# One-column steps, low parts on GpSimd and the order of work at the ends of sub-layers, in a two-layer fp32 trunk on one core

## The chip, the core and the metric

The kernel runs on one core of a Trainium2 chip. A core has TensorE (matrix products; the profile lists its weight loads apart, as PEld), VectorE (DVE), ScalarE (ACT), GpSimd (POOL) and SyncE (SP), which issues DMAs. SBUF is the memory of 128 partitions that the engines work in; PSUM is the one that TensorE accumulates in. The metric is the device time of one execution in microseconds. A VectorE operation that takes a tensor and, for each partition, one number from a column of SBUF is called a tensor-scalar step here; `scalar_tensor_tensor` takes two tensors and such a scalar.

## The reference

The input is 256 frames of 2048 numbers, all fp32. Four sub-layers follow each other, each of the form x <- x + RMSNorm_post(f(RMSNorm_pre(x))):

```python
for layer in range(DEPTH):                       # DEPTH = 2
    h = rms_norm(x, mix_pre_g[layer])
    m = pool_conformer_mixer(...) if layer % 2 == 0 else short_conv_mixer(...)
    x = x + rms_norm(m, mix_post_g[layer])
    h = rms_norm(x, ffn_pre_g[layer])
    x = x + rms_norm(sq_relu_mlp(h, ffn_w1[layer], ffn_w2[layer]), ffn_post_g[layer])
```

rms_norm is y = x * rsqrt(mean(x*x) + 1e-6) * g. The first mixer projects to 3072 columns, pools and convolves over time and projects back with `ab_w_out`; the second projects to 6144 columns, convolves over three frames between two gates and projects back with `sc_w_out`. The MLP is (relu(h W1))^2 W2 with 8192 hidden columns. Most of the work is these products with fp32 weights, which are read from HBM once.

## The kernel before

**Tiling.** The 256 frames are two row blocks, t = 0 and 1, of 128 rows on the partitions. A product works on an output block of 512 columns: one PSUM bank `pg`, into which TensorE sums over the 128-row slices k of the contraction. The left operand of a matmul is a slice of the transposed input, the right one 512 columns of a weight.

**Split products.** Weights and inputs are split into a high part of fewer bits and the rest. For each k three matmuls are issued: high weight by high input (line 216), low weight by high input (217), high weight by low input (218). Such a loop over the 16 slices of a segment (one weight block of 2048 x 512, eight loads) is 48 matmuls for each row block.

**Weight stream.** `prep_to` (lines 166 to 176) brings the weights in, two slices k at a time: a DMA on SyncE into `raw` (four buffers), a cast on ScalarE into `whi`, and the subtraction raw - whi (line 174) into `wlo`, nine buffers each. The subtraction runs on VectorE; for the first nine loads of the three segments that open MLP 0, mixer 1 and MLP 1 (`f1_0_0_0`, `sC0`, `f1_1_0_0`), which `pool_lo` holds, on GpSimd. A load waits until the low part that read its buffer four loads earlier is done.

**End of a sub-layer.** The output blocks of a row block are evacuated from PSUM one by one. In the mixers `mix_evac` sums the squares on ScalarE (line 555) and multiplies by the gain of the post-norm (`gp`, an own DMA) on VectorE (line 556); in the first mixer two blocks are added from halves first (line 611). In the MLP the eight groups of hidden columns are added up in SBUF (line 664), and the last addition is followed by the squares and the product with the gain (lines 669, 671). Then `mix_close` and `rsqrt` make the scale of the row on [128, 1] columns: a reduction and a step (269, 561), `scalar_tensor_tensor` of the last square sum with the others (564), a root on ScalarE and a reciprocal (289), and one Newton step for it (291, 292, 293). `close_row` adds scale times block to the residual x in four pieces (line 319) and queues, behind some more slices of matrix products (`later`), `norm_chunk` for each of the four pieces: four transposes on TensorE (line 245), the high part `xh` on ScalarE (231), the low part `xl` on VectorE (234). These eight-slice buffers `xh`, `xl` are the left operands of the next sub-layer's first segment, which row block 0 enters as soon as row block 1's last block is done. A "chunk" below is one of these four pieces, k = 0 to 3, 4 to 7, 8 to 11, 12 to 15. Each row's pre-norm scale `rr` is worked out later (`row_scale`) and applied when the products leave PSUM.

**Order of the work.** The kernel is written for one stream of instructions on each engine, each in order; the framework's scheduler simulates a timeline of the program as it is built and sets the order in which the instructions of an engine stand from the order of the code, their priority and the simulated times. An engine waits at the head of its queue until the inputs are there; SyncE's DMAs are in such a queue too.

## Time and profile before

| | before |
|---|---|
| median of 3 runs | 2096.06 us (2094.62 to 2098.18) |
| span of the profiled execution | 2096.0 us |
| TensorE (PE) busy | 2048.8 us, 98%, 9253 instructions |
| VectorE (DVE) busy | 1187.4 us, 57% |
| ScalarE (ACT) busy | 1007.8 us, 48% |
| GpSimd (POOL) busy | 221.5 us, 11% |
| bytes moved by DMA | 390.31 MB, mean 186 GB/s |
| TensorE's mean granted clock | 0.992 |

The profile is that of one execution, whose own time is its span; times in it count from its first instruction. A row says on which engine and line of the kernel something ran and on which tiles (the numbers behind their names are left out). Where an engine stood idle, the row behind names what ended the wait, as far as the semaphores show it. A matmul of 512 columns is shown with a length of 0.39 us while the next one starts before it has ended, so a busy share of TensorE near 100% says that it hardly waits. The granted clock is that share of full speed at which TensorE was allowed to run.

### The profile page before, as it was taken

The numbers are of one execution on the slowest core, as the hardware profiler recorded it, in microseconds if no ns is written. First come the engines' busy times: TensorE is split into PE (matmuls) and PEld (weight loads), VectorE is DVE, ScalarE is ACT, GpSimd is POOL, SyncE is SP. The second block draws the span as 40 slices with busy tenths as digits, with TensorE's granted clock in tenths as the row PEclk, the third lists the DMA queues.
The fourth block names the chain that finished last, engine by engine and source line by source line (L and its number), as shares of the span: only waits on it lengthen the run. The fifth ranks groups of instructions, "written<-read, shape, count | busy, mean of one in ns | idle before, by whom it ended". The sixth has DMA issues, their size and how long they took to land.

```text
span 2096.0 us, 24559 instructions
## 1 busy us (share of the span) xinstructions
PE 2048.8 (98%) x9253; PEld 1693.0 (81%) x9253; DVE 1187.4 (57%) x1494; ACT 1007.8 (48%) x1296; POOL 221.5 (11%) x111
## 2 busy tenths in 40 slices
PE   8999889999999999999999999989999999999998
PEld 7888778888888888887788888878888888888886
DVE  4787765445454555546655655565455454454545
ACT  7454565445344354444643444465444444354443
POOL 5886210000000000002100000220000000000000
PEclk9999999999999999999999999999999999999999
DMA  7665445556565555555555565546556565565553
GB/s 259 197 208 174 151 161 191 190 171 206 196 196 171 196 186 196 189 173 170 174 199 180 182 204 181 191 156 212 180 178 211 174 201 186 175 202 199 192 170 120
DMA packets 203079, 390.31 MB, mean 186 GB/s; under 512 B 12368, under 2 KB 14512, under 8 KB 202960
## 3 DMA queue, kind: packets, MB, share of 16 engines
q1 hardware_dynamic: 202656, 388.55, 56.3%
q8 instruction: 72, 1.18, 0.2%
q14 instruction: 47, 0.39, 0.1%
q0 software_dynamic: 256, 0.18, 0.0%
q10 hardware_dynamic: 48, 0.02, 0.0%
HBM read 386.60 MB, written 2.10 MB: 185 GB/s over the span
## 4 chain that ended last, share of the span: by engine, by line
PE 84%; DVE 3%; DMA 1%; ACT 0%; issue 0%; DVEq 0%; SPq 0%; ACTq 0%
PE pg L218 27%; PE pg L216 27%; PE pg L217 27%; PE pt L245 2%; DVE x L319 1%; DVE sm L291 0%; DVE sm L293 0%; DMA gp<-in_mix_post_g_dram 0%; DMA raw<-in_ab_w_out_dram 0%; DVE sm L564 0%; DMA raw<-in_ffn_w_dram 0%; DMA raw<-in_sc_w_in_dram 0%; DVE m L556 0%; ACT whi L173 0%; DVE m L671 0%
## 5 line engine op out<-in xcount | busy, mean ns | idle before, releaser
L174 DVE TENSOR_TENSOR wlo<-raw,whi 128x1024 fp32r<-128x1024 f32 x633 | 775.4, 1227 | 583.9 <-ACT whi L173 550.3
L173 ACT CAST whi<-raw 128x1024 fp32r<-128x1024 f32 x722 | 760.1, 1054 | 581.8 <-PE pg L218 381.8
L218 PE MATMUL pg<-whi,xl 128*128 128x512 f32 x1568 | 618.5, 395 | 17.9 <-DVE xl L234 17.9
L216 PE MATMUL pg<-whi,xh 128*128 128x512 f32 x1568 | 612.6, 392 | 1.3 <-ACT xh L231 0.7
L217 PE MATMUL pg<-wlo,xh 128*128 128x512 f32 x1568 | 612.2, 391 | 0.0
L217 PE MATMUL pg<-wlo,ah 128*128 128x512 f32 x1024 | 399.2, 390 | 0.0
L216 PE MATMUL pg<-whi,ah 128*128 128x512 f32 x1024 | 398.7, 389 | 0.0
L218 PE MATMUL pg<-whi,al 128*128 128x512 f32 x1024 | 398.2, 391 | 0.0
L218 PEld LDWEIGHTS pg<-whi,xl 128*128 128x128 f32 x1568 | 295.8, 189 | 79.0 <-DVE xl L234 20.1
L217 PEld LDWEIGHTS pg<-wlo,xh 128*128 128x128 f32 x1568 | 295.8, 189 | 61.7
L216 PEld LDWEIGHTS pg<-whi,xh 128*128 128x128 f32 x1568 | 295.9, 189 | 61.1 <-ACT xh L231 1.7
L174 POOL TENSOR_TENSOR wlo<-raw,whi 128x1024 fp32r<-128x1024 f32 x89 | 214.3, 2435 | 1012.4 <-DVE wlo L174 693.8
L217 PEld LDWEIGHTS pg<-wlo,ah 128*128 128x128 f32 x1024 | 192.6, 188 | 40.2
L216 PEld LDWEIGHTS pg<-whi,ah 128*128 128x128 f32 x1024 | 192.6, 188 | 39.5
L218 PEld LDWEIGHTS pg<-whi,al 128*128 128x128 f32 x1024 | 192.5, 188 | 39.3
L634 ACT ACTIVATE t<-pg,rr 128x512 f32<-128x512 f32 x64 | 43.8, 685 | 190.6 <-PE pg L218 190.6
L664 DVE TENSOR_TENSOR m<-pg,m 128x512 f32<-128x512 f32 x112 | 76.9, 686 | 89.4 <-PE pg L218 89.4
L216 PE MATMUL pg<-whi,yh 128*128 128x512 f32 x256 | 101.2, 396 | 1.6 <-ACT yh L240 1.5
L217 PE MATMUL pg<-wlo,yh 128*128 128x512 f32 x256 | 100.9, 394 | 0.0
L218 PE MATMUL pg<-whi,yl 128*128 128x512 f32 x256 | 98.8, 391 | 0.2 <-DVE yl L241 0.2
L385 DVE SCALAR_TENSOR_TENSOR acc<-pp,par,acc 128x256 f32<-128x256 f32 x240 | 96.3, 479 | 0.1
L241 DVE TENSOR_TENSOR al<-pt,ah 128x512 fp32r<-128x512 f32 x64 | 44.0, 687 | 71.8 <-ACT ah L240 71.7
(124 smaller groups left out, 858.8 us busy)
## 6 DMA issues: line engine op xcount, KB each, us to landing
raw<-in_ffn_w_dram SPq DMA_DIRECT2D x512, 512.0 KB, 4.7
raw<-in_sc_w_in_dram SPq DMA_DIRECT2D x96, 512.0 KB, 4.8
raw<-in_ab_w_in_dram SPq DMA_DIRECT2D x48, 512.0 KB, 4.4
raw<-in_ab_w_out_dram SPq DMA_DIRECT2D x32, 512.0 KB, 3.9
raw<-in_sc_w_out_dram SPq DMA_DIRECT2D x32, 512.0 KB, 5.4
x<-in_x_dram SPq DMA_DIRECT2D x8, 256.0 KB, 7.7
gp<-in_mix_post_g_dram SPq DMA_DIRECT2D x8, 256.0 KB, 6.2
gp<-in_ffn_post_g_dram SPq DMA_DIRECT2D x8, 256.0 KB, 4.3
```

What stands on the lines that cost most here:

```text
L173: act.copy(hi, raw)
L174: (pool if nxt[0] in pool_lo else lo_eng[0](nxt[0])).tensor_tensor(lo, raw, hi.bitcast(F32), ALU.subtract)
L216: pe.matmul(ps, lh, wh, start=start and k == 0, stop=False)
L217: pe.matmul(ps, lh, wl, start=False, stop=False)
L218: pe.matmul(ps, ll, wh, start=False, stop=stop and k == n - 1)
L241: dve.tensor_tensor(lo, src, hi.bitcast(F32), ALU.subtract)
L245: pe.transpose(p[:, j * P : (j + 1) * P], src[:, j * P : (j + 1) * P], ident)
L319: dve.scalar_tensor_tensor(xs[t][:, cs], ms[t][:, cs], s, xs[t][:, cs], ALU.mult, ALU.add)
L385: dve.scalar_tensor_tensor(a, src, wcol, a, ALU.mult, ALU.add)
L634: act.activation(rl, ps, AF.Relu, scale=rr[t])
L664: dve.tensor_tensor(dst, ps, dst, ALU.add)
```

## The change

Five things are changed; the computation is the same.

- Lines 564, 291 and 293, one-column steps of two SBUF tensors, become tensor-scalar steps whose other operand is a scalar column (600, 322, 324 in the new numbering).
- `pool_lo` holds every second load of the three opening segments (four of the first eight or nine), and such a low part is worked out in two instructions of 512 columns; the other loads' low parts run on VectorE.
- The last group of an MLP block is added up in PSUM, squared from PSUM and multiplied from PSUM into SBUF (`last_evac`). The program's very last product, which was on GpSimd, is on VectorE too.
- `urgent` gives the instructions of the evacuation, of `mix_close` with the residual sums, and of `norm_chunk` a priority of 150 over the others, which the scheduler heeds.
- In the first segment behind each of the three ends, row block 0 runs through `mms_wide`: high by high and high by low for all k first (lines 240, 241), then low by high for all k (248).

```diff
     for key in ("f1_0_0_0", "sC0", "f1_1_0_0"):
-        pool_lo |= set(range(seg[key][0], seg[key][0] + 9))
+        pool_lo |= set(seg[key][1::2])
     wt = {}
...
             act.copy(hi, raw)
-            (pool if nxt[0] in pool_lo else lo_eng[0](nxt[0])).tensor_tensor(lo, raw, hi.bitcast(F32), ALU.subtract)
-            wt[nxt[0]] = (hi, lo)
+            i_, on_pool = nxt[0], nxt[0] in pool_lo
+            def low(raw=raw, hi=hi, lo=lo, on_pool=on_pool, eng=lo_eng[0](i_)):
+                for s in ((slice(0, CB), slice(CB, 2 * CB)) if on_pool else (slice(None),)):
+                    (pool if on_pool else eng).tensor_tensor(
+                        lo[:, s], raw[:, s], hi.bitcast(F32)[:, s], ALU.subtract)
+            low()
+            wt[i_] = (hi, lo)
             nxt[0] += 1
...
     AHEAD = 8
+    URGENT = 150
...
+    def mms_wide(ps, lhs, ids):
+        n = 2 * len(ids)
+        prep_to(ids[-1])
+        for i, c in enumerate(ids):
+            if i == n // 4:
+                tick()
+            for j in range(2):
+                k = 2 * i + j
+                wh = wt[c][0][:, j * CB : (j + 1) * CB]
+                lh, ll = lhs(k)
+                pe.matmul(ps, lh, wh, start=k == 0, stop=False)
+                pe.matmul(ps, ll, wh, start=False, stop=False)
+        tick()
+        for i, c in enumerate(ids):
+            if i == n // 4:
+                tick()
+            for j in range(2):
+                k = 2 * i + j
+                pe.matmul(ps, lhs(k)[0], wt[c][1][:, j * CB : (j + 1) * CB],
+                          start=False, stop=k == n - 1)
+        tick()
     def ahead(ids, t):
...
         h = small()
-        dve.scalar_tensor_tensor(h, y, v, y, ALU.mult, ALU.mult)
+        dve.tensor_scalar(h, y, v, y, ALU.mult, ALU.mult)
         dve.tensor_scalar(h, h, -0.5, 1.5, ALU.mult, ALU.add)
-        dve.tensor_tensor(y, y, h, ALU.mult)
+        dve.tensor_scalar(y, y, h, None, ALU.mult)
         return y
...
     ms, rr, nparts = {}, {}, {}
+    def urgent(fn, *args):
+        with tc.high_priority(URGENT):
+            fn(*args)
...
             else:
-                later(2 + (c + 1) // 2, lambda c=c: norm_chunk(t, c, *nxt_gain))
-
+                later(2 + (c + 1) // 2, lambda c=c: urgent(norm_chunk, t, c, *nxt_gain))
     for t in range(NT):
...
         v = small()
-        dve.scalar_tensor_tensor(v, last, 1.0 / D, base, ALU.mult, ALU.add)
+        dve.tensor_scalar(v, last, 1.0 / D, base, ALU.mult, ALU.add)
         r = rsqrt(v, root=lambda s: act.activation(s, last, AF.Sqrt, bias=base, scale=1.0 / D))
...
             ps = o
-        mix_evac(t, cb, ps, gps[cb], parts)
+        urgent(mix_evac, t, cb, ps, gps[cb], parts)
         if cb == 1:
-            mix_close(t, parts, ("ffn_pre", 0))
-
+            urgent(mix_close, t, parts, ("ffn_pre", 0))
+    def last_evac(t, cb, ps, gp, parts):
+        dst = ms[t][:, cb * CB : (cb + 1) * CB]
+        dve.tensor_tensor(ps, ps, dst, ALU.add)
+        junk = tp.tile([P, CB], BF16, tag="junk", name=nm("junk"), bufs=2)
+        act.activation(junk, ps, AF.Square, accum_out=parts[t][:, cb : cb + 1])
+        dve.tensor_tensor(dst, ps, gp, ALU.mult)
     def ffn(l, nxt_gain, final=False):
...
                     ps = psg()
-                    mms(ps, lhs_x(t), ids, 0, True, True)
+                    if (e, c, t) == (0, 0, 0):
+                        mms_wide(ps, lhs_x(t), ids)
+                    else:
+                        mms(ps, lhs_x(t), ids, 0, True, True)
                     rl = t512()
...
                     continue
-                dve.tensor_tensor(dst, ps, dst, ALU.add)
-                if last:
-                    if cb not in gps:
-                        gps[cb] = post_gain(ffn_post_g, l, cb)
-                    junk = tp.tile([P, CB], BF16, tag="junk", name=nm("junk"), bufs=2)
-                    act.activation(junk, dst, AF.Square, accum_out=parts[t][:, cb : cb + 1])
-                    eng = pool if final and (cb, t) == (NCB - 1, NT - 1) else dve
-                    eng.tensor_tensor(dst, dst, gps[cb], ALU.mult)
-                    if cb == NCB - 1:
-                        mix_close(t, parts, nxt_gain, final)
+                if not last:
+                    dve.tensor_tensor(dst, ps, dst, ALU.add)
+                    continue
+                if cb not in gps:
+                    gps[cb] = post_gain(ffn_post_g, l, cb)
+                urgent(last_evac, t, cb, ps, gps[cb], parts)
+                if cb == NCB - 1:
+                    urgent(mix_close, t, parts, nxt_gain, final)
...
                 ps = psg()
-                mms(ps, lhs_x(t), ids, 0, True, True)
+                if (j, key, t) == (0, "C", 0):
+                    mms_wide(ps, lhs_x(t), ids)
+                else:
+                    mms(ps, lhs_x(t), ids, 0, True, True)
                 if key == "C":
...
             mms(ps, lhs_y(t), ids, 0, True, True)
-            mix_evac(t, cb, ps, gp, parts)
+            urgent(mix_evac, t, cb, ps, gp, parts)
             if cb == NCB - 1:
-                mix_close(t, parts, ("ffn_pre", KT))
+                urgent(mix_close, t, parts, ("ffn_pre", KT))
```

The names in the order below are tiles with their numbers. VectorE at the end of the first mixer, before: the last product of row block 0 (`m_2077`), its root's steps, the four residual sums (`x_85`), then row block 1 (`m_2078`) and the first `xl` of MLP 0.

```order
L556 TENSOR_TENSOR m_2077<-opart_1807,gp_2294 128x512
L564 SCALAR_TENSOR_TENSOR sm_2353<-parts_2075,sm_2349 128x1
L289 RECIPROCAL sm_2357<-sm_2355 128x1
L291 SCALAR_TENSOR_TENSOR sm_2359<-sm_2357,sm_2353 128x1
L292 TENSOR_SCALAR sm_2359<-sm_2359 128x1
L293 TENSOR_TENSOR sm_2357<-sm_2357,sm_2359 128x1
L319 SCALAR_TENSOR_TENSOR x_85<-m_2077,sm_2357,x_85 128x512 x4
L611 TENSOR_TENSOR opart_1810<-pg_2371,opart_1810 128x512
L556 TENSOR_TENSOR m_2078<-opart_1810,gp_2263 128x512
L269 TENSOR_REDUCE sm_2506<-parts_2076 128x1
L561 TENSOR_SCALAR sm_2505<-sm_2506 128x1
L234 SCALAR_TENSOR_TENSOR xl_2364<-pt_2396,par,xh_2363 128x128 x4
```

The same place after, in two pieces that follow each other:

```order
L600 TENSOR_SCALAR sm_2355<-parts_2075,sm_2351 128x1
L320 RECIPROCAL sm_2359<-sm_2357 128x1
L322 TENSOR_SCALAR sm_2361<-sm_2359,sm_2355 128x1
L323 TENSOR_SCALAR sm_2361<-sm_2361 128x1
L324 TENSOR_SCALAR sm_2359<-sm_2359,sm_2361 128x1
L178 TENSOR_TENSOR wlo_2312<-raw_2309,whi_2311 128x1024
L355 SCALAR_TENSOR_TENSOR x_85<-m_2077,sm_2359,x_85 128x512 x4
L647 TENSOR_TENSOR opart_1810<-pg_2373,opart_1810 128x512
L178 TENSOR_TENSOR wlo_2418<-raw_2415,whi_2417 128x1024
```

```order
L592 TENSOR_TENSOR m_2078<-opart_1810,gp_2263 128x512
L300 TENSOR_REDUCE sm_2510<-parts_2076 128x1
L597 TENSOR_SCALAR sm_2509<-sm_2510 128x1
L178 TENSOR_TENSOR wlo_2431<-raw_2428,whi_2430 128x1024
L647 TENSOR_TENSOR opart_1810<-pg_2441,opart_1810 128x512
L265 SCALAR_TENSOR_TENSOR xl_2366<-pt_2398,par,xh_2365 128x128 x4
L592 TENSOR_TENSOR m_2078<-opart_1810,gp_2294 128x512
L265 SCALAR_TENSOR_TENSOR xl_2366<-pt_2454,par,xh_2365 128x128 x4
L178 TENSOR_TENSOR wlo_2542<-raw_2539,whi_2541 128x1024
L600 TENSOR_SCALAR sm_2513<-parts_2076,sm_2509 128x1
L265 SCALAR_TENSOR_TENSOR xl_2368<-pt_2467,par,xh_2367 128x128 x4
```

Between the root's steps and the low parts of chunk 0 (`xl_2366` from `pt_2398`), of chunk 1 (from `pt_2454`) and of chunk 2 (`xl_2368`) there are now four low parts of weights (`wlo_...`), and the three one-column steps carry the new operation.

TensorE where MLP 0's first segment begins, before: three matmuls for each slice k.

```order
L216 MATMUL pg_2559<-whi_2298,xh_2363 128x512
L217 MATMUL pg_2559<-wlo_2299,xh_2363 128x512
L218 MATMUL pg_2559<-whi_2298,xl_2364 128x512
L216 MATMUL pg_2559<-whi_2304,xh_2363 128x512
L217 MATMUL pg_2559<-wlo_2305,xh_2363 128x512
L218 MATMUL pg_2559<-whi_2304,xl_2364 128x512
L216 MATMUL pg_2559<-whi_2304,xh_2363 128x512
L217 MATMUL pg_2559<-wlo_2305,xh_2363 128x512
L245 MATMUL pt_2463<-ident,x_85 128x128 x4
L218 MATMUL pg_2559<-whi_2304,xl_2364 128x512
```

The same after: two for each slice, the low parts of the weights not yet among them.

```order
L240 MATMUL pg_2563<-whi_2298,xh_2365 128x512
L241 MATMUL pg_2563<-whi_2298,xl_2366 128x512
L240 MATMUL pg_2563<-whi_2298,xh_2365 128x512
L241 MATMUL pg_2563<-whi_2298,xl_2366 128x512
L240 MATMUL pg_2563<-whi_2304,xh_2365 128x512
L241 MATMUL pg_2563<-whi_2304,xl_2366 128x512
L240 MATMUL pg_2563<-whi_2304,xh_2365 128x512
L276 MATMUL pt_2467<-ident,x_85 128x128 x4
L241 MATMUL pg_2563<-whi_2304,xl_2366 128x512
L240 MATMUL pg_2563<-whi_2311,xh_2365 128x512
```

The transposes of chunk 2 (`pt_2463`, `pt_2467`) stand behind eight matmuls before and behind seven after; by then the matmuls have come to the third slice k in one case and to the fourth in the other.

SyncE behind the first end, before: weight loads (`raw_...`) and the loads of the next post-norm gain (`gp_...`).

```order
L170 DMA raw_2425<-in_ffn_w_dram 128x2x512
L304 DMA gp_7499<-in_ffn_post_g_dram 128x512
L170 DMA raw_2431<-in_ffn_w_dram 128x2x512
L170 DMA raw_2535<-in_ffn_w_dram 128x2x512
L304 DMA gp_7554<-in_ffn_post_g_dram 128x512
```

After:

```order
L170 DMA raw_2428<-in_ffn_w_dram 128x2x512
L170 DMA raw_2434<-in_ffn_w_dram 128x2x512
L170 DMA raw_2539<-in_ffn_w_dram 128x2x512
L340 DMA gp_7502<-in_ffn_post_g_dram 128x512
L170 DMA raw_2545<-in_ffn_w_dram 128x2x512
```

The first gain load stands behind two weight loads more than before.

## Rows read from the trace of the kernel before

**Rows 1.** The list of waits of TensorE over the whole span: engine and line that waited <- what it waited for: us in total, times, longest.

```profile
PE pg L218 <- DVE xl L234: 17.9, 5, 7.3
PE pt L245 <- DVE x L319: 7.7, 3, 4.2
```

**Rows 2.** Busy time of the engines in three windows (us from the span's start), at the ends of the first three sub-layers. Columns: window, its length, then busy us and instructions of PE, PEld, DVE, ACT and POOL, the granted TensorE clock as a share of full speed, the DMA engines' share, GB/s.

```profile
256.00:310.00 54.00, 43.57 (x188) 34.81 (x187) 40.21 (x77) 30.87 (x73) 14.29 (x6) 0.91 0.47 152
970.00:1035.00 65.00, 56.39 (x246) 45.12 (x245) 47.89 (x87) 37.11 (x83) 21.92 (x11) 0.95 0.52 163
1340.00:1410.00 70.00, 62.72 (x288) 51.47 (x287) 47.59 (x80) 39.98 (x84) 22.94 (x9) 0.95 0.55 174
```

**Rows 3.** The same three windows, the transposes of line 245 alone (PE and PEld busy us and instructions, clock, DMA share, GB/s).

```profile
256.00:310.00 54.00, 6.62 (x36) 5.44 (x36) 0.91 0.47 152
970.00:1035.00 65.00, 5.31 (x32) 4.13 (x32) 0.95 0.52 163
1340.00:1410.00 70.00, 5.99 (x40) 5.05 (x40) 0.95 0.55 174
```

**Rows 4.** The timeline of TensorE around the first end and, for the transposes, around the third. Columns: start us, us, engine, line, operation, out<-in, count [idle time before it <- what ended it]; "x4" is four instructions shown as one row, from the start of the first to the end of the last. Matmuls are pipelined, so the distance from start to start, not the length, is what one takes.

```profile
236.66 0.39 PE L217 MATMUL pg<-wlo,yh 128*128 128x512 f32 x1
...
246.86 0.39 PE L217 MATMUL pg<-wlo,yh 128*128 128x512 f32 x1
...
279.54 0.80 PE L218 MATMUL pg<-whi,xl 128*128 128x512 f32 x1 [5.71 <-DVE xl L234]
280.13 0.63 PE L216 MATMUL pg<-whi,xh 128*128 128x512 f32 x1
280.56 0.63 PE L217 MATMUL pg<-wlo,xh 128*128 128x512 f32 x1
...
1358.58 0.60 PE L245 MATMUL pt<-ident,x 128*128 128x128 f32 x4
...
1359.24 0.39 PE L218 MATMUL pg<-whi,yl 128*128 128x512 f32 x1
```

**Rows 5.** The timeline of VectorE at the first end, same columns.

```profile
248.19 0.69 DVE L611 TENSOR_TENSOR opart<-pg,opart 128x512 f32<-128x512 f32 x1 [1.02 <-PE pg L218]
251.06 2.60 DVE L556 TENSOR_TENSOR m<-opart,gp 128x512 f32<-128x512 f32 x1 [2.18 <-DMA gp<-in_mix_post_g_dram]
253.59 2.35 DVE L564 SCALAR_TENSOR_TENSOR sm<-parts,sm 128x1 f32<-128x1 f32 x1
...
256.05 2.22 DVE L291 SCALAR_TENSOR_TENSOR sm<-sm,sm 128x1 f32<-128x1 f32 x1
258.30 0.15 DVE L292 TENSOR_SCALAR sm<-sm 128x1 f32<-128x1 f32 x1
258.49 2.08 DVE L293 TENSOR_TENSOR sm<-sm,sm 128x1 f32<-128x1 f32 x1
260.60 2.74 DVE L319 SCALAR_TENSOR_TENSOR x<-m,sm,x 128x512 f32<-128x512 f32 x4
```

**Rows 6.** The timeline of GpSimd at the first end, same columns.

```profile
250.72 9.84 POOL L174 TENSOR_TENSOR wlo<-raw,whi 128x1024 fp32r<-128x1024 f32 x4 [4.34 <-ACT whi L173]
```

**Rows 7.** The timeline of VectorE at the second end, same columns.

```profile
978.68 0.69 DVE L664 TENSOR_TENSOR m<-pg,m 128x512 f32<-128x512 f32 x1 [1.53 <-PE pg L218]
...
981.56 2.12 DVE L291 SCALAR_TENSOR_TENSOR sm<-sm,sm 128x1 f32<-128x1 f32 x1
...
986.08 6.91 DVE L319 SCALAR_TENSOR_TENSOR x<-m,sm,x 128x512 f32<-128x512 f32 x4
```

**Rows 8.** The timeline of VectorE at the third end, same columns.

```profile
1353.34 9.16 DVE L319 SCALAR_TENSOR_TENSOR x<-m,sm,x 128x512 f32<-128x512 f32 x4
```

**Rows 9.** All instructions of line 383, grouped: duration in ns as minimum/median/maximum, first and last start, form.

```profile
L383 DVE TENSOR_SCALAR acc<-pp,par x8: 537/544/547, 65.8 to 124.3; 128x256 f32<-128x256 f32 x8
```

**Rows 10.** The page: line 174 on VectorE and on GpSimd among the costliest groups (count | busy us, mean ns of one | idle before, releaser), and the loads of the MLP weights among the DMA issues (count, KB each, median us from issue to landing).

```profile
L174 DVE TENSOR_TENSOR wlo<-raw,whi 128x1024 fp32r<-128x1024 f32 x633 | 775.4, 1227 | 583.9 <-ACT whi L173 550.3
...
L174 POOL TENSOR_TENSOR wlo<-raw,whi 128x1024 fp32r<-128x1024 f32 x89 | 214.3, 2435 | 1012.4 <-DVE wlo L174 693.8
...
raw<-in_ffn_w_dram SPq DMA_DIRECT2D x512, 512.0 KB, 4.7
```

**Rows 11.** The timeline of ScalarE at the first end, columns as in rows 4.

```profile
270.79 1.05 ACT L173 CAST whi<-raw 128x1024 fp32r<-128x1024 f32 x1 [2.14 <-DMA raw<-in_ffn_w_dram]
271.74 0.62 ACT L555 ACTIVATE junk<-opart 128x512 bf16<-128x512 f32 x1
```

**Rows 12.** The timeline of SyncE's DMA issues at the first end (a row lasts from the first issue to the last).

```profile
264.69 0.34 SPq L304 DMA_DIRECT2D gp<-in_ffn_post_g_dram  x1
265.13 0.90 SPq L170 DMA_DIRECT2D raw<-in_ffn_w_dram  x2
```

**Rows 13.** The timeline of TensorE at the second end, columns as in rows 4.

```profile
996.75 0.50 PE L218 MATMUL pg<-whi,xl 128*128 128x512 f32 x1 [0.43 <-DVE xl L234]
...
1008.44 0.59 PE L218 MATMUL pg<-whi,xl 128*128 128x512 f32 x1 [4.06 <-DVE xl L234]
```

**Rows 14.** The timeline of TensorE at the third end.

```profile
1362.65 0.39 PE L216 MATMUL pg<-whi,xh 128*128 128x512 f32 x1
...
1376.95 0.79 PE L218 MATMUL pg<-whi,xl 128*128 128x512 f32 x1 [7.28 <-DVE xl L234]
```

**Rows 15.** The timeline of VectorE at the program's end.

```profile
2088.13 0.85 DVE L291 SCALAR_TENSOR_TENSOR sm<-sm,sm 128x1 f32<-128x1 f32 x1
```

## The prediction

> **What bounds the kernel now.** I read first the page's busy shares, then who waits for whom on TensorE, then the three stretches in which it waits, and last what VectorE does there. TensorE is busy 98% of the span and its chain is nearly the whole program, so only its idle and slow time can be won. The list of its waits shows two large groups [rows 1]: 17.9 us for `xl` of VectorE line 234 (the low part of the next sub-layer's input) and 7.7 us for `x` of line 319 (the residual sum). All of it lies where one sub-layer closes and the next begins: mixer 0 to MLP 0 (first end, near 255 us), MLP 0 to mixer 1 (second, near 985), mixer 1 to MLP 1 (third, near 1360).
>
> What these ends lose in all is the length of their stretches less the matmuls at full speed. A 512-column matmul takes 0.227 us from start to start (45 from 236.66 to 246.86), and four transposes add 0.44 (0.66 from the four to the second matmul behind them, less 0.227) [rows 4]. With the counts of [rows 2, 3]: 54.0 - 152 x 0.227 - 9 x 0.44 = 15.5; 65.0 - 214 x 0.227 - 8 x 0.44 = 12.9; 70.0 - 248 x 0.227 - 10 x 0.44 = 9.3. Sum 37.7 us: the 25.6 of waits, and the rest the clock. Behind the wait that ends at 279.54 the matmuls start 0.43 apart, the lower of the two clock levels [rows 4].
>
> Why VectorE is late: at the first end a one-column step with two SBUF tensors takes 2.35, 2.22 and 2.08 us, while the one-input step between them takes 0.15 [rows 5]. GpSimd runs four low parts of 2.4 us back to back at that time [rows 6], and each slow step ends where one of these ends. So a VectorE instruction with two SBUF inputs waits out the GpSimd instruction that is running. The same shows in the residual sums: four take 2.74 without GpSimd [rows 5], 6.91 and 9.16 with it [rows 7, 8].
>
> **The change, part by part.** *One-column steps.* Lines 564, 291, 293 become one-input steps with the other columns as scalars. Line 383 has that form (one SBUF tensor, two column scalars) and all eight ran in 0.54 us for 256 columns, spread from 65.8 to 124.3 us [rows 9]; 0.15 is the row for a column. I take 0.15 to 0.22. Bounds: 0.15 and the 2.35 of today. At the first end that takes 6.1 us out of row block 0's chain (2.35 + 2.22 + 2.08 - 0.52), at the second about 3.9 (two steps like the 2.12 at 981.56 [rows 7]).
>
> *Four low parts on GpSimd, each in halves.* GpSimd's 2.44 us [rows 10] becomes two instructions; by their size, 1.2 each is my estimate. What a residual sum still waits is thus at most 1.2, not 2.4. But five of nine low parts go to VectorE at 1.23 each [rows 10], and the order shows four of them between the root and the `xl` of chunks 0 to 2, on the very engine that TensorE waits for.
>
> *MLP blocks summed in PSUM.* Line 671 read two SBUF tensors; the new product reads PSUM and one SBUF tensor, a form of 0.69 (line 611 in [rows 5], 664 in [rows 7]). The sum is of the same form as before. Cover: nothing waits for the product but the residual sum; it costs nothing more than now.
>
> *Chain first.* The transposes of row block 0's first two chunks stand 5 matmuls later at the first and second end, 45 matmuls (10.2 us [rows 4]) behind its last block. And SP: a gain load that waited for VectorE stood ahead of weight loads (issued 264.69, the weights at 265.13, their cast at 270.79 held the square sum behind it [rows 11, 12]). Now these weights stand ahead of it.
>
> *Two phases.* The first segment's 48 matmuls ask for a new chunk of `xl` every 8 matmuls instead of every 12, and need no low part for the first 32. Matmul count unchanged.
>
> Now each end by hand, from the last matmul of row block 0.
> First end: TensorE is done at 248.2; the gain row lands at 251 as now [rows 5], since what frees its buffer has not moved. Product (0.69, and up to 1.2 for GpSimd), four small steps (0.7): 253.6, against 260.6 now. Then a low part (1.23), four sums (2.7, with one or two waits of up to 1.2): 258 to 260. TensorE transposes at 248.2 + 10.2 = 258.4 without a wait, and 8 transposes and 3 matmuls later, at 260.0, starts the new segment. But VectorE still has a sum of block 1, a low part, a product, a low part and a sum ahead of the first `xl`: 0.6 + 1.23 + 0.69 + 1.23 + 0.6 and one GpSimd half, 5 us: 264.5. Wait 4.3 us. Chunk 2's `xl` stands behind a low part whose weights are loaded into the buffer that the low part at 260 frees: load 4.7 [rows 10], cast 1.05 [rows 11], square sum 0.6, low part 1.2, 268.5 to 270, and TensorE comes there at 264.5 + 16 x 0.227 + 0.9 = 269. Wait 0.5. Block 1's sums then lie under the 16 matmuls of the second phase; its first `xh` costs some 0.7. The lower clock behind a wait of this size: 1.4 (7 slots of 0.2 more). Left: 6.9 of 15.5.
> Second end: done at 978.7 [rows 7]; product, root and steps 982 instead of 986; a low part behind its cast 984; sums 987 to 989; TensorE transposes at 988.9, no wait. The first `xl` has two low parts, two sums and a product ahead of it, each pair behind a cast: 993.5 to 995 (996.75 now [rows 13]), TensorE ready at 990.6: wait 3.6. Chunk 2 comes at about 999, as TensorE does; before, it came at 1008.44. With 0.7 and 1.4 more and 0.9 for what chunk 2 may be late: 6.6 of 12.9.
> Third end: the chain was not slowed, the sums were (9.16). With halves they end at about 1359.3 (1362.5 now [rows 8]); two low parts behind them bring the first `xl` to where it is now, in time. TensorE begins the segment at 1362.65 as now (its wait of 7.28 comes 26 matmuls later) [rows 14] and wants chunk 2 after 16 matmuls and eight transposes, at 1367.2. That stands behind a load into the buffer that the second of the two low parts frees, at 1361.8: load 4.7, three casts and a square sum (3.8), `xh` and `xl` 0.6: 1370.9. Wait 3.7; with 0.7 and the clock 1.4: 5.8 of 9.3.
> Sum left: 19.3 of 37.7, a gain of 18.4. The program's end: line 291 took 0.85 beside GpSimd's last product [rows 15]; without GpSimd it is 0.2, but the product (0.69) now stands on VectorE ahead of the reciprocal and delays it by about 0.35. Gain 0.3. The profiled execution spans 2096.0, the median of the runs is 2096.06, so no correction: 2096.0 - 18.7 = 2077.
>
> A place where the Trainium skill speaks against the change: "SBUF — State Buffer", section "Who interferes with whom", says that `tensor_scalar` too can run in a mode that takes the port pair shared with GpSimd, if its operands meet certain conditions. [...]
>
> **The rivals.** *All is covered.* If the low parts on VectorE find their casts done and slip into gaps, only the latency of the first `xl` and `xh` is left, about 1.2 an end: 37.7 - 3.6 = 34 gained, 2062. For it: VectorE idles some 25% of these stretches [rows 2]. Against: its order is fixed, and the low parts stand ahead. 0.15.
> *Low parts give it back.* If each of the four low parts ahead of an `xl` waits a full GpSimd half as well (1.2 each, 4.8 an end, of which the forecast has 1.2): 3 x 3.6 = 11 less, 2088. 0.14.
> *The new steps still wait.* Seven stalled steps (three, two, two) at 1.2 each: 8.4 less, 2085. 0.04.
> *Slower.* A low part waits for a cast, this for a load, this for the buffer that an earlier low part frees. If that loop stands once more ahead of each first `xl` than I count, it costs 1.23 + 4.7 + 1.05 = 7 us an end and by my estimate 2 of clock (ten slots of 0.2): 27 more than 2077, 2104. It decides from 6.2 us an end on (18.7 / 3). Against: the buffers of chunks 0 and 1 are loaded before the end begins. 0.03. Two thirds of that loop is no change: 2095, 0.05.
>
> **How the numbers follow.** The forecast as worked out, 2070 to 2084, has 0.59; all covered 0.15, given back 0.14, steps still wait 0.04, no change 0.05, slower 0.03. The range 2064 to 2090 leaves out most of the first rival's far end, no change and slower: about 0.2 with half of the covered case. A measurement of this kernel tells 0.2% (4.2 us) from no change: faster means under 2092. Faster 0.92, same 0.05, slower 0.03.
>
> **What would show it.** In the profile after: the three one-column steps at 0.15 to 0.22 wherever GpSimd runs; no wait of TensorE for `x`; the largest wait for the first `xl` at the first two ends, 3 to 5 us; at the third a wait of 2 to 4 for chunk 2; residual sums of four in 3 to 6 us, never 9. Wrong if a one-column step still takes over 1 us, if TensorE waits for a low part of GpSimd in the second phase, or if it waits over 6 us for one chunk.

## The result, and the profile after

The changed kernel takes 2083.74 us (median of 4 runs, 2083.05 to 2086.29) against 2097.03 for the kernel before (4 runs, 2094.62 to 2098.18): a ratio of 0.9945, 95% interval 0.9931 to 0.9959. It is faster by 0.55%, 11.5 us by the ratio and 13.3 by the medians. The forecast of 2077 asked for 18.7; the range, 2064 to 2090, holds the time. The profiled execution of the changed kernel took 2086.29 with a span of 2084.5, so about 1.8 us lie around the span.

The list of TensorE's waits (what waited <- for what: us, times, longest), to be held against [rows 1]:

```profile
PE pg L241 <- DVE xl L265: 9.1, 4, 4.5
PE pg L240 <- ACT xh L262: 5.8, 3, 2.2
...
PE pg L224 <- ACT xh L262: 2.3, 3, 0.8
```

The wait for the residual sum (7.7 us) is gone, and that for `xl` has fallen from 17.9 to 9.1. New is a wait for `xh`, the high part from ScalarE: 8.1 in all, where before it had 0.7; 5.8 of that is row block 0's (line 240), each time with a wait for `xl` right behind it.

The three windows, all of TensorE and the transposes (line 276) alone, as in [rows 2, 3]:

```profile
256.00:310.00 54.00, 46.55 (x214) 37.87 (x213) 38.41 (x77) 32.66 (x76) 8.52 (x5) 0.94 0.55 175
970.00:1035.00 65.00, 59.83 (x267) 48.81 (x266) 44.99 (x89) 37.15 (x80) 12.84 (x10) 0.95 0.48 158
1340.00:1410.00 70.00, 65.43 (x296) 53.17 (x295) 47.26 (x87) 43.49 (x88) 12.53 (x8) 0.95 0.49 157
```

```profile
256.00:310.00 54.00, 6.13 (x40) 5.24 (x40) 0.94 0.55 175
970.00:1035.00 65.00, 4.93 (x32) 4.25 (x32) 0.95 0.48 158
1340.00:1410.00 70.00, 6.27 (x44) 5.34 (x44) 0.95 0.49 157
```

With the prediction's formula the ends now lose 54.0 - 174 x 0.227 - 10 x 0.44 = 10.1, 65.0 - 235 x 0.227 - 8 x 0.44 = 8.1 and 70.0 - 252 x 0.227 - 11 x 0.44 = 8.0 us: 26.2 instead of 37.7. So 11.5 us were won, all of it at the ends; 6.9, 6.6 and 5.8 had been forecast to be left.

VectorE at the first end (start, us, line, operation; compare [rows 5]):

```profile
250.76 1.73 DVE L592 TENSOR_TENSOR m<-opart,gp 128x512 f32<-128x512 f32 x1 [1.95 <-DMA gp<-in_mix_post_g_dram]
252.41 0.20 DVE L600 TENSOR_SCALAR sm<-parts,sm 128x1 f32<-128x1 f32 x1
...
252.72 0.27 DVE L322 TENSOR_SCALAR sm<-sm,sm 128x1 f32<-128x1 f32 x1
...
253.22 0.21 DVE L324 TENSOR_SCALAR sm<-sm,sm 128x1 f32<-128x1 f32 x1
253.35 1.38 DVE L178 TENSOR_TENSOR wlo<-raw,whi 128x1024 fp32r<-128x1024 f32 x1
254.65 4.80 DVE L355 SCALAR_TENSOR_TENSOR x<-m,sm,x 128x512 f32<-128x512 f32 x4
259.36 0.68 DVE L647 TENSOR_TENSOR opart<-pg,opart 128x512 f32<-128x512 f32 x1
259.96 2.07 DVE L178 TENSOR_TENSOR wlo<-raw,whi 128x1024 fp32r<-128x1024 f32 x1
261.95 1.76 DVE L592 TENSOR_TENSOR m<-opart,gp 128x512 f32<-128x512 f32 x1
...
263.89 2.24 DVE L178 TENSOR_TENSOR wlo<-raw,whi 128x1024 fp32r<-128x1024 f32 x1
266.05 0.68 DVE L647 TENSOR_TENSOR opart<-pg,opart 128x512 f32<-128x512 f32 x1
266.65 1.11 DVE L265 SCALAR_TENSOR_TENSOR xl<-pt,par,xh 128x128 fp32r<-128x128 f32 x4
```

GpSimd and ScalarE there:

```profile
250.64 6.93 POOL L178 TENSOR_TENSOR wlo<-raw,whi 128x512 fp32r<-128x512 f32 x4 [48.27 <-ACT whi L173]
259.69 3.47 POOL L178 TENSOR_TENSOR wlo<-raw,whi 128x512 fp32r<-128x512 f32 x2 [2.12 <-ACT whi L173]
263.78 3.48 POOL L178 TENSOR_TENSOR wlo<-raw,whi 128x512 fp32r<-128x512 f32 x2 [0.62 <-ACT whi L173]
```

```profile
260.08 0.63 ACT L591 ACTIVATE junk<-opart 128x512 bf16<-128x512 f32 x1 [0.47 <-DVE opart L647]
...
260.71 1.03 ACT L173 CAST whi<-raw 128x1024 fp32r<-128x1024 f32 x1
261.64 1.13 ACT L262 ACTIVATE xh<-pt,par 128x128 fp32r<-128x128 f32 x4
```

And TensorE, first at the first and then at the third end:

```profile
262.05 0.50 PE L240 MATMUL pg<-whi,xh 128*128 128x512 f32 x1 [2.19 <-ACT xh L262]
...
267.04 0.80 PE L241 MATMUL pg<-whi,xl 128*128 128x512 f32 x1 [4.50 <-DVE xl L265]
...
1359.85 0.49 PE L240 MATMUL pg<-whi,xh 128*128 128x512 f32 x1 [1.89 <-ACT xh L262]
...
1361.86 0.79 PE L241 MATMUL pg<-whi,xl 128*128 128x512 f32 x1 [1.51 <-DVE xl L265]
1362.45 0.63 PE L240 MATMUL pg<-whi,xh 128*128 128x512 f32 x1
...
1366.71 0.63 PE L240 MATMUL pg<-whi,xh 128*128 128x512 f32 x1
```

The reader is to see four things. The one-column steps take 0.20 to 0.27 us while GpSimd runs. Each instruction with two SBUF tensors that meets a GpSimd half is about 1 us longer (2.07 and 2.24 for low parts that take 1.24 on average, 1.76 for a product). The first `xl` (266.65) has two such low parts and such a product right ahead of it. And the first `xh` stands on ScalarE behind a square sum, which had waited for VectorE, and a cast, though its transposes began at 258.13. That lateness costs nothing of its own: VectorE works nearly without a pause from 259.36 to the first `xl`, so TensorE would have stood there until 267.04 with an earlier `xh` too.

### The profile page after: what moved, and what is told of

It is laid out like the page before. It is cut to its first block, busy times and chain, and to the rows that moved or that the text cites. A ratio compares the mean times of both kernels' runs of the same rounds, so it can differ in the third digit from the quotient of the medians.

```text
span 2084.5 us, 24569 instructions
## 1 busy us (share of the span) xinstructions
PE 2046.8 (98%) x9253; PEld 1693.3 (81%) x9253; DVE 1177.6 (56%) x1510; ACT 1005.7 (48%) x1296; POOL 192.6 (9%) x107
## 4 chain that ended last, share of the span: by engine, by line
PE 85%; DVE 2%; DMA 1%; ACT 1%; issue 0%; DVEq 0%; SPq 0%; ACTq 0%
PE pg L224 27%; PE pg L226 27%; PE pg L225 27%; PE pt L276 2%; DVE x L355 1%; DVE wlo L178 1%; PE pg L241 1%; PE pg L240 0%; PE pg L248 0%; DMA gp<-in_mix_post_g_dram 0%; DMA raw<-in_ab_w_out_dram 0%; ACT whi L173 0%; DVE m L592 0%; DMA raw<-in_ffn_w_dram 0%; ACT junk L307 0%
## 5 line engine op out<-in xcount | busy, mean ns | idle before, releaser
L178 DVE TENSOR_TENSOR wlo<-raw,whi 128x1024 fp32r<-128x1024 f32 x648 | 799.5, 1237 | 582.6 <-ACT whi L173 549.4
L226 PE MATMUL pg<-whi,xl 128*128 128x512 f32 x1520 | 596.3, 393 | 0.0
L224 PE MATMUL pg<-whi,xh 128*128 128x512 f32 x1520 | 591.2, 390 | 2.7 <-ACT xh L262 2.3
L225 PE MATMUL pg<-wlo,xh 128*128 128x512 f32 x1520 | 591.7, 390 | 0.0
L224 PEld LDWEIGHTS pg<-whi,xh 128*128 128x128 f32 x1520 | 285.7, 188 | 60.4 <-ACT xh L262 3.0
L225 PEld LDWEIGHTS pg<-wlo,xh 128*128 128x128 f32 x1520 | 285.6, 188 | 59.0
L226 PEld LDWEIGHTS pg<-whi,xl 128*128 128x128 f32 x1520 | 285.6, 188 | 56.8
L178 POOL TENSOR_TENSOR wlo<-raw,whi 128x1024 fp32r<-128x1024 f32 (+1 forms) x86 | 186.8, 2204 | 1020.0 <-ACT whi L173 1019.4
L711 DVE TENSOR_TENSOR m<-pg,m 128x512 f32<-128x512 f32 x96 | 65.9, 687 | 72.2 <-PE pg L226 72.2
```

Of the source, the lines that this page charges most:

```text
L178: (pool if on_pool else eng).tensor_tensor(lo[:, s], raw[:, s], hi.bitcast(F32)[:, s], ALU.subtract)
L224: pe.matmul(ps, lh, wh, start=start and k == 0, stop=False)
L225: pe.matmul(ps, lh, wl, start=False, stop=False)
L226: pe.matmul(ps, ll, wh, start=False, stop=stop and k == n - 1)
L711: dve.tensor_tensor(dst, ps, dst, ALU.add)
```

## The experiments

The theory after reading the result: the *place* of a few instructions in VectorE's and ScalarE's queues decides what TensorE waits for, together with the time that VectorE and GpSimd hold each other up. The rivals: the new steps cost time by themselves; the two phases ask for the chunks too early; the low parts on VectorE are the load. All kernels, with the loss of the three ends from the same formula. Each ratio is to runs of the kernel before that were made beside the kernel (medians 2095.57 to 2097.03). The losses are those of one execution each, and ahead of the first end executions already differ: VectorE's addition of row block 0's last product, 248.19 in [rows 5], starts between 246.15 (a4) and 249.25 (b2).

| kernel | us | ratio to before, 95% | ends lose, us | sum |
|---|---|---|---|---|
| before | 2097.03 | | 15.5, 12.9, 9.3 | 37.7 |
| changed | 2083.74 | 0.9945 (0.9931 to 0.9959) | 10.1, 8.1, 8.0 | 26.2 |
| a1: before + steps | 2086.48 | 0.9954 (0.9942 to 0.9966) | 8.8, 9.5, 9.1 | 27.4 |
| a2: changed, old steps | 2076.81 | 0.9911 (0.9898 to 0.9923) | 6.2, 5.4, 5.2 | 16.8 |
| a3: nine low parts, halves | 2086.11 | 0.9961 (0.9947 to 0.9974) | 9.0, 9.3, 8.0 | 26.3 |
| a4: nine low parts, whole | 2089.60 | 0.9970 (0.9958 to 0.9982) | 9.3, 9.7, 10.9 | 29.9 |
| d1: short chain | 2079.97 | 0.9924 (0.9912 to 0.9937) | 8.1, 5.7, 6.6 | 20.4 |
| d2: d1 + PSUM in mixer 0 | 2077.39 | 0.9914 (0.9901 to 0.9927) | 6.0, 6.1, 6.6 | 18.7 |
| b1: no two phases | 2078.51 | 0.9916 (0.9903 to 0.9929) | 8.7, 5.2, 3.9 | 17.8 |
| b2: no priority | 2084.85 | 0.9947 (0.9936 to 0.9959) | 10.8, 8.1, 8.4 | 27.3 |
| b4: MLP sums in SBUF | 2086.32 | 0.9953 (0.9939 to 0.9966) | 10.1, 9.3, 7.7 | 27.1 |
| e1: d2, no two phases | 2070.79 | 0.9878 (0.9865 to 0.9892) | 4.0, 3.8, 3.6 | 11.4 |
| f1: e1, old steps | 2072.19 | 0.9886 (0.9870 to 0.9903) | 5.8, 4.1, 4.1 | 14.0 |
| f2: e1, whole low parts | 2071.87 | 0.9886 (0.9872 to 0.9901) | 5.8, 3.2, 4.1 | 13.1 |

**a1: the steps alone.**

```diff
-        dve.scalar_tensor_tensor(h, y, v, y, ALU.mult, ALU.mult)
+        dve.tensor_scalar(h, y, v, y, ALU.mult, ALU.mult)
...
-        dve.tensor_tensor(y, y, h, ALU.mult)
+        dve.tensor_scalar(y, y, h, None, ALU.mult)
...
-        dve.scalar_tensor_tensor(v, last, 1.0 / D, base, ALU.mult, ALU.add)
+        dve.tensor_scalar(v, last, 1.0 / D, base, ALU.mult, ALU.add)
```

> The kernel before with nothing but the three one-column steps (lines 564, 291, 293) as tensor-scalar steps. Theory: only instructions with two SBUF tensors wait for GpSimd, so the steps take 0.15 to 0.27 us; but the four residual sums behind them now start 6 us earlier at the first end, under GpSimd's whole low parts, and wait there as they do at the third end (9.16). So little reaches TensorE: 2 to 3 us at the first end, 1 to 2 at the second, nothing at the third: 2091 to 2094. Rival: the steps were the whole delay, 6.1 and 3.9 us come back in full: 2086.

2086.48, the rival's number, but not for the rival's reason. By its interval the kernel can't be told from the whole change. VectorE in this kernel:

```profile
250.00 10.23 DVE L319 SCALAR_TENSOR_TENSOR x<-m,sm,x 128x512 f32<-128x512 f32 x4
...
270.39 1.13 DVE L234 SCALAR_TENSOR_TENSOR xl<-pt,par,xh 128x128 fp32r<-128x128 f32 x4
271.44 4.87 DVE L319 SCALAR_TENSOR_TENSOR x<-m,sm,x 128x512 f32<-128x512 f32 x4
```

and in the kernel before:

```profile
275.06 4.16 DVE L319 SCALAR_TENSOR_TENSOR x<-m,sm,x 128x512 f32<-128x512 f32 x3
279.15 1.11 DVE L234 SCALAR_TENSOR_TENSOR xl<-pt,par,xh 128x128 fp32r<-128x128 f32 x4
```

The four sums do wait, as the theory said: 10.23 us, against 2.74 in [rows 5], so the 6 us of the steps hardly reach TensorE through them. What was won is chunk 2's low part: it stood behind row block 1's sums (279.15, TensorE's 5.71 us of [rows 4]) and now stands ahead of them (270.39). The three edits changed the order in which the scheduler put the instructions, and at the first end that brought most of the gain. At the second the wait for chunk 2, 4.06 in [rows 13], became 1.45; what made it so was not followed up.

**a2: all of the change but the steps** (the diff above, reversed).

> The changed kernel with the three one-column steps as they were before. Theory: each of them waits for a running half of a GpSimd low part again, about 1 us each, three at the first end and two at the second, none on row block 0's chain at the third: 2 to 5 us slower than the changed kernel, 2086 to 2089. Rival: they stand under cover, since the first low part of the input waits for weights' low parts and casts whatever the steps take: no difference, 2083 to 2085.

Both were wrong: 2076.81, 7 us *faster* than the changed kernel. The old steps do wait (0.96 and 1.03 us at the first end), but the order is another one. VectorE and ScalarE in this kernel, as the program orders them, to be held against the changed kernel's order of VectorE ahead of the prediction:

```
L324 TENSOR_TENSOR sm_2359<-sm_2359,sm_2361 128x1
L355 SCALAR_TENSOR_TENSOR x_85<-m_2077,sm_2359,x_85 128x512 x4
L178 TENSOR_TENSOR wlo_2312<-raw_2309,whi_2311 128x1024
...
L265 SCALAR_TENSOR_TENSOR xl_2366<-pt_2398,par,xh_2365 128x128 x4
```

```
L591 ACTIVATE junk_2412,parts_2076<-opart_1810 128x512
L262 ACTIVATE xh_2365<-pt_2398,par 128x128 x4
L262 ACTIVATE xh_2365<-pt_2454,par 128x128 x4
L173 CAST whi_2430<-raw_2428 128x1024
L173 CAST whi_2436<-raw_2434 128x1024
```

and ScalarE in the changed kernel:

```
L591 ACTIVATE junk_2412,parts_2076<-opart_1810 128x512
L173 CAST whi_2430<-raw_2428 128x1024
L262 ACTIVATE xh_2365<-pt_2398,par 128x128 x4
L173 CAST whi_2436<-raw_2434 128x1024
L262 ACTIVATE xh_2365<-pt_2454,par 128x128 x4
```

What VectorE and TensorE then do in this kernel:

```profile
252.03 4.82 DVE L355 SCALAR_TENSOR_TENSOR x<-m,sm,x 128x512 f32<-128x512 f32 x4
256.77 1.21 DVE L178 TENSOR_TENSOR wlo<-raw,whi 128x1024 fp32r<-128x1024 f32 x1
...
262.06 1.11 DVE L265 SCALAR_TENSOR_TENSOR xl<-pt,par,xh 128x128 fp32r<-128x128 f32 x4
```

```profile
259.65 0.49 PE L240 MATMUL pg<-whi,xh 128*128 128x512 f32 x1 [1.00 <-ACT xh L262]
...
262.45 0.50 PE L241 MATMUL pg<-whi,xl 128*128 128x512 f32 x1 [2.30 <-DVE xl L265]
```

The sums come ahead of the weights' low part, the first `xl` (262.06) ahead of the third one (`wlo_2431`), both `xh` ahead of two casts. TensorE's first two waits are 1.00 and 2.30 instead of 2.19 and 4.50. The first `xl` follows VectorE's work without a pause here too, so it is VectorE's order that counts at this end. That holds for the first two ends, which lose 6.6 us less than in the changed kernel. At the third, VectorE's order and nearly the waits for chunk 2 (1.54 and 1.51) are the changed kernel's; the 2.8 us less go with the granted clock, 1.00 instead of 0.95. The gain row `gp` came earlier as well: the product of row block 0 waited 0.50 us for it instead of 1.95; d1 below has the same order with the late row. Why the scheduler turned these places round for three short steps isn't shown by a run.

**a3 and a4: nine low parts on GpSimd, in halves and whole.** a3 puts `range(seg[key][0], seg[key][0] + 9)` back into `pool_lo`; a4 also has one instruction for a low part.

> The changed kernel with all of the first nine low parts of the three segments on GpSimd again, in halves. Theory: at the ends VectorE's low parts of weights stand ahead of the first low part of the input and wait for GpSimd's halves, as these wait for them; with none of them on VectorE TensorE's waits for the first low part of the input (4.5, 2.7 and 1.5 us in the changed kernel) fall to under 1.5 each: 2077 to 2081. Rival: GpSimd's 2.5 us a load is now the pace at which weight buffers come free, casts come late and TensorE waits for high parts of weights or for the second phase's low parts: 2086 to 2092.

> The changed kernel with all of the first nine low parts on GpSimd, each in one instruction, as before the change. Theory: a residual sum waits for up to a whole low part of 2.4 us, not a half of 1.3, so four sums under GpSimd take 7 to 9 us, not 5 to 6: 2 to 3 us an end slower than with nine halves, 2083 to 2088. Rival: GpSimd is busy as long in sum, so halving makes no difference: within 1 us of nine halves.

2086.11 and 2089.60. With no low part on VectorE the first `xl` is indeed early, but another wait takes its place, and neither theory had it (a3, VectorE and TensorE):

```profile
266.54 6.03 DVE L355 SCALAR_TENSOR_TENSOR x<-m,sm,x 128x512 f32<-128x512 f32 x4
272.49 1.11 DVE L265 SCALAR_TENSOR_TENSOR xl<-pt,par,xh 128x128 fp32r<-128x128 f32 x4
```

```profile
272.89 0.50 PE L241 MATMUL pg<-whi,xl 128*128 128x512 f32 x1 [4.41 <-DVE xl L265]
```

Row block 1's four sums, each beside a GpSimd half, stand ahead of chunk 3. It is again an order, with the price of the halves on top. Whole low parts lose 3.6 us more at the ends, 2.9 of it at the third, and a4 lies above its theory's range; the intervals of the times overlap.

**d1 and d2: new steps in the good order.** The Newton step is rewritten so that one step less stands behind the reciprocal, which the scheduler answers with a2's order at the first end. d2 also adds up mixer 0's last blocks in PSUM.

```diff
+        hv = small()
+        dve.tensor_scalar(hv, v, -0.5, None, ALU.mult)
...
-        dve.tensor_scalar(h, y, v, y, ALU.mult, ALU.mult)
-        dve.tensor_scalar(h, h, -0.5, 1.5, ALU.mult, ALU.add)
-        dve.tensor_scalar(y, y, h, None, ALU.mult)
+        dve.tensor_scalar(h, y, hv, y, ALU.mult, ALU.mult)
+        dve.tensor_scalar(y, h, 1.5, y, ALU.add, ALU.mult)
```

```diff
-            dve.tensor_tensor(o, ps, o, ALU.add)
-            ps = o
+            dve.tensor_tensor(ps, ps, o, ALU.add)
```

> The changed kernel with the Newton step in two one-column steps behind the reciprocal instead of three (minus half of v is formed beside the root). The scheduler then puts the residual sums ahead of the weights' low part, and the first xh and xl ahead of casts and low parts, as it did when the three steps were undone (2076.8), while the steps stay free of GpSimd. Theory (order decides): the changed kernel's extra loss against that run came from the order, so this one has its good order and saves the two stalled steps of about 1 us besides: 2072 to 2076. Rival (the tensor-scalar steps themselves cost time, through the port or in some other way): as slow as the changed kernel, 2081 to 2085.

> As the short chain, and the first mixer's last blocks are also added up in PSUM and multiplied from there, so that the product has one SBUF tensor. Theory: this product took 1.7 instead of 0.7 us under a running GpSimd half, twice ahead of the first low part of the input at the first end: 1 to 2 us faster than the short chain, all at the first end. Rival: the order of the queues shifts again and takes it back: within 1 us.

d1 takes 2079.97, between theory and rival; its interval just meets the changed kernel's (0.9937 and 0.9931). TensorE at its first end:

```profile
260.64 0.50 PE L240 MATMUL pg<-whi,xh 128*128 128x512 f32 x1 [1.22 <-ACT xh L262]
263.44 0.80 PE L241 MATMUL pg<-whi,xl 128*128 128x512 f32 x1 [2.29 <-DVE xl L265]
```

These are a2's waits, though the gain row kept mixer 0's last product waiting for 2.08 us, as in the changed kernel: the order makes them short, not the row. At the ends 5.8 us less are lost than in the changed kernel, so the order is most of the difference, but d1 isn't faster than a2. Part of that is the gain row: from the start of that product to the first residual sum d1 takes 2.57 us and a2 3.93, but a2's product waited only 0.50. d2 gives 2077.39, 2.6 us less than d1, and its 2.1 at the first end are where the theory put them; 0.9924 and 0.9914 have overlapping intervals.

**b1: without the two phases.** Row block 0's first segments go through `mms` again.

> The changed kernel without the two phases: the first segments run three matmuls a slice again. Theory: a chunk then lasts 12 matmuls instead of 8, so the waits for the later chunks shrink, but low parts of the weights are wanted from the second matmul on and GpSimd's halves and VectorE's low parts for loads 2 to 8 come late: 1 to 4 us slower than the changed kernel, 2085 to 2088. Rival: the first xl is late whatever the phase, and eight matmuls' more time a chunk help: 1 to 3 us faster, 2081 to 2083.

2078.51: the rival, and by more than it said. The windows:

```profile
256.00:310.00 54.00, 48.01 (x220) 39.02 (x219) 38.47 (x78) 34.86 (x79) 7.26 (x5) 0.94 0.53 170
970.00:1035.00 65.00, 61.77 (x282) 50.42 (x281) 47.77 (x89) 40.12 (x83) 13.56 (x10) 0.97 0.52 171
1340.00:1410.00 70.00, 67.13 (x316) 54.50 (x315) 48.85 (x83) 45.72 (x90) 10.79 (x8) 1.00 0.57 184
```

At the third end 3.9 us are lost instead of 8.0 and the granted clock is 1.00 instead of 0.95. The phases with 8 matmuls a chunk run into chunk 2 before ScalarE and VectorE have it (the 1.89 and 1.51 above), and behind this wait the matmuls stand 0.43 apart from 1362.45 to 1366.71, the lower clock level. With 12 matmuls a chunk, and the same order on VectorE up to there at all three ends, chunk 2 is waited for 0.37 and 1.31 us at the third end, and the clock stays up. a2, which has the phases, shows 1.00 there as well, so the fall of the clock isn't the phases' alone. The weights' low parts, wanted from the second matmul on, are no wait that the list of TensorE's waits has.

**b2 and b4: without the priority; MLP blocks in SBUF.** b2 calls the functions without `tc.high_priority`; b4 lets `last_evac` write the sum to SBUF and square and multiply from there.

> The changed kernel without the higher priority. The order at the first end shows hardly a difference on VectorE. Theory: the priority decides nothing where the scheduler's simulated times leave only one ready instruction: within 2 us of the changed kernel, 2082 to 2086. Rival: the chain first is what the change lives from: 2088 or more.

> The changed kernel with the last MLP blocks added up into SBUF, squared and multiplied from there, as before. TensorE's order is the same word for word. Theory: the product with two SBUF tensors waits for a GpSimd half where one runs, that is for row block 1 at the second end, once or twice, and delays the first low part of the input there by 1 us or so: 0 to 2 us slower than the changed kernel, 2083 to 2086. Rival: the sum into PSUM and the square behind it are what is slow: 1 us or more faster, under 2083.

b2, 2084.85, can't be told from the changed kernel: the priority decides nothing measurable here. b4, 2086.32, is 0.3 above its theory's range, and the interval overlaps too; its second end loses 1.2 us more, and the product in question takes 1.76 there instead of 0.68.

**e1, f1, f2: the parts put together.** e1 is d2 without the two phases; f1 has the three old steps in place of e1's short chain (and the order of a2); f2 is e1 with GpSimd's low parts in one instruction.

> The short chain and the PSUM sums in the first mixer, without the two phases. Theory: leaving out the two phases gave 5 us from the changed kernel's order, most of it at the second and third end (5.61 and 4.22 us lost there instead of 8.55 and 8.30), because a chunk then lasts 12 matmuls and not 8; the better order gave 4 to 6 us on its own. Both concern the same waits, so they add up only in part: 2071 to 2075. Rival: with the better order chunks come early enough and the two phases no longer cost anything, or even help: 2076 to 2079, as the short chain with PSUM sums (2077.4).

> The best version so far (2070.8) with the three one-column steps as before the change, in an order that still puts the sums first and the first xh and xl ahead of the third weights' low part. Theory: in the same order the old steps cost what they wait for a GpSimd half, two of about 1 us and 0.2 for the step that the short chain saves, at the first end and part of it at the second: 1 to 4 us slower than the best version, 2072 to 2075. Rival: the steps are under cover there too: within 1 us.

> The best version so far with GpSimd's four low parts in one instruction each. Theory: a residual sum or low part on VectorE waits for up to 2.4 us instead of 1.3, but half as often, so that four sums take about as long and the longest single wait is 1.1 longer: 0 to 3 us slower, 2071 to 2074. Rival: whole low parts make VectorE late at each end as they did with nine of them (2089.6 against 2086.1), 3 us or more: 2074 to 2078.

e1 takes 2070.79, 1.2% less than before and 0.7% less than the changed kernel, and just under its theory's range. (The 5.61, 4.22, 8.55 and 8.30 of its expectation are 0.3 to 0.4 above the same losses in the table.) TensorE's waits:

```profile
PE pg L226 <- DVE xl L265: 6.0, 8, 1.3
...
PE pg L224 <- ACT xh L262: 1.3, 3, 0.5
```

At the ends none is longer than 1.3. The two gains add up nearly in full: from the changed kernel's 26.2 the better order with PSUM takes 7.5, leaving out the phases 8.4, both 14.8. f1 and f2 are 1.4 and 1.1 us slower, inside their theories' ranges, with intervals that overlap e1's. So in a good order the two items that the prediction had weighed most, the steps and the halves, bring little or nothing that can be measured, although the traces show each of them doing what it should.

## Why the prediction was right, and where its sum failed

That the time fell into the range is in part luck. Two of the parts that were counted as help, the steps and the two phases, each make the finished kernel slower (a2 and b1 are 7 and 5 us faster without them), and a1, the steps alone, can't be told from the whole change. Which part carries the 11.5 us isn't shown: no kernel here that lacks one of them went back to the time before.

- **What bounds the kernel**: right. All that was won lies in the three windows; elsewhere the two traces lose the same.
- **One-column steps**: size about right (0.15 to 0.22 forecast, 0.20 to 0.27 measured beside GpSimd), so the rival that they still wait fell. The section of the Trainium skill that was weighed there ("SBUF — State Buffer", "Who interferes with whom") lets `tensor_scalar` contend only where its operands meet the conditions of a 2-port mode; it doesn't say that a one-column step would wait, and in this trace none did. Their worth was wrong: a1, a2 and f1 show that what they bring or take comes through the order.
- **Halves**: 1.2 estimated; one alone takes 1.26 at least. What failed is "one GpSimd half" as the price of the five instructions ahead of the first `xl`, 5 us in all (5.55 by its own terms). They took 7.3 (259.36 to 266.65): three of them waited, 0.84, 1.07 and 1.0. The product was counted in the form that reads PSUM, 0.69, but in mixer 0 it reads two SBUF tensors. Here the rival "low parts give it back" was right in kind; with all four low parts paying it would have been 2088, and the time lies between.
- **GpSimd waits as well**, which the prediction had left out: a half that meets a low part on VectorE takes up to 2.3 (3.47 for two, one of them free). The same page of the Trainium skill says so ("SBUF: two separate sides"): the port pair is an exclusive lock, which whoever starts first holds for the whole instruction while the other is blocked. This trace agrees: 2.25 behind a low part, 1.26 alone.
- **`xh`**: 0.7 an end was allowed, for row block 1, and measured (2.3 for three). TensorE also waited 2.2, 1.7 and 1.9 for `xh` of row block 0, because casts and a square sum stand ahead of it on ScalarE, an order that could be read before. But each of these is followed by a wait for `xl` (4.5, 2.7 and 1.5), whose place behind low parts on VectorE decided when TensorE went on, so they are no loss of their own.
- **Two phases**: taken as help ("a new chunk every 8 matmuls", no low part for the first 32). Undoing them alone gave 8.4 us at the ends, 5.2 in time (b1). The wait at the third end was forecast (3.7; 1.9 + 1.5 measured), as was its cause, but it was booked against the change as a whole and not against the phases.
- **Low clock**: 1.4 an end; at the third the matmuls stood 0.43 apart for 4.3 us, about 10 slots of 0.2, 2.0. Over the three ends the waits come to 17.2 (9.1 + 5.8 + 2.3) of the 26.2 lost, where the forecast had 15.1 of 19.3; the rest, which the prediction puts down to the clock, is 9.0 instead of 4.2. So of the 6.9 us that the sum was short, 4.8 lie in this term and 2.1 in waits. About 30 slots of 0.2 instead of 21 make 6 of the 9.0; what the remainder is stays open.
- **MLP blocks in PSUM, priority**: forecast at nothing on the path; b4 and b2 show nothing that can be told apart from it.
- **The program's end**: 0.3 forecast. From the last sum to the last residual sum it took 5.99 (2074.80 to 2080.79) against 6.14 (2086.12 to 2092.26) before: 0.15.

Not tried: the four halved low parts on GpSimd with nothing else changed, all low parts on VectorE, and an earlier load of the gain row.

## What to carry to other kernels

When several engines with in-order queues meet at a serial step, read the place of the two or three instructions that the bounding engine waits for in each queue, before and after, before adding up durations: here the order was worth most of a2's 7 us, and the durations that the change removed 1.4 and 1.1 in the good order, within the intervals (f1, f2). An edit that makes an instruction cheaper also gives the scheduler other times to order by; so undo each part alone in the finished kernel, since a part that helps the old order can hurt the new one. Of two phases of a product, ask how fast the first wants its inputs and whether the engines that make them can keep up.

## What the runs showed of the hardware that was not expected

A VectorE instruction with two SBUF tensors and a GpSimd instruction hold each other up in both directions: residual sums of 0.75 take 1.78 and halves of 1.27 take 1.74 when they alternate, a whole low part on VectorE makes a half up to 2.3. Halving GpSimd's instructions therefore shortens the longest wait, and the sum of them only where GpSimd runs low part after low part: with nine low parts there four sums took 5.85 us beside halves (a3) and 10.23 beside whole ones (a4), with only four 6.05 (e1) and 6.19 (f2), at the first end. And the load of a gain row, which decides when mixer 0's chain begins, kept the product waiting for 2.18 us in the kernel before [rows 5], 1.95 in the changed one, 0.52 in a1 and 0.50 in a2, with the same order of DMAs up to there: some 1.5 us of an end hang on when this transfer lands, and what decides that isn't shown.
